# Low parts of the weights by an accumulating DMA instead of a VectorE subtraction

## The chip, the cores and the metric

The kernel runs on one core of one Trainium2 chip. The metric is the device time of one execution in microseconds (us); a verdict compares medians of several runs. The engines are named as the profile names them: PE (TensorE matmul) and PEld (its weight load), DVE (VectorE), ACT (ScalarE), POOL (GpSimd), SP (SyncE, which here issues loads and stores).

## The reference

One inference step of a diffusion backbone with two layers. 128 context tokens and 512 latent tokens go through the same weights. Each layer is a feed-forward sublayer, a token mixer (differential attention in layer 0, a gated linear recurrence called HGRN in layer 1) and a second feed-forward sublayer; each has an RMSNorm before and after it and a modulation (shift, scale, gate) made from `w_mod`. Everything is fp32. What matters here are the products with large weights:

```
D_MODEL = 1024;  FFN_HIDDEN = 2816
def swiglu(h, w_in, w_out):
    a, b = jnp.split(h @ w_in, 2, axis=-1)
    return (jax.nn.silu(a) * b) @ w_out
...
z = h @ w_in                                            # attention 1024 x 3072, HGRN 1024 x 5120
y = o.reshape(B, L, DA_HEADS * DA_DV) @ w_out           # 1024 x 1024, both mixers
```

## The kernel before

The 640 tokens stand as columns, in two groups of NG = 320, and features lie on the 128 partitions. To hold fp32 accuracy with matmuls in the faster fp32r format, each weight w and each activation x is split into a rounded high part and a low part that is the difference. A product is the sum of three: w_hi x_hi and w_hi x_lo (both line 315) and w_lo x_hi (line 320). One matmul covers 128 rows of weight, 128 output columns and 320 tokens.

A `Unit` is a slab of weights with 128 output columns and 1024 rows (896 for most of the FFN's `w_out`), 512 KB (448 KB). A `Job` multiplies a unit with one group or with both: 24 matmuls for each group, in the order 315, 315, 320 for each 128 rows (with both groups each of these twice). Jobs with both groups fill most of the FFNs. Jobs with one group stand where a stage begins or ends: an "FFN head" (`ffn_head`, 16 units, all for group 0 and then for group 1 in reverse), an "FFN tail" (`split`, the last 8 units of `w_out`, group 0 and then group 1), and many of the mixers' products.

A unit passes through three steps. `ensure_dma` (line 231) loads its raw fp32 slab on SP's queue into a ring of RAW_BUFS = 3 tiles `wraw`. `convert` makes the high part by a rounding copy on ACT (line 249) and the low part by a subtraction on DVE (line 250), into a tile `whl` of a ring of HL_BUFS = 3, or into free space of the large tensors H or G ("hosted" units). `prepare` calls `convert` up to AHEAD = 3 jobs before a job needs it, as far as the ring has room. A raw tile is free again when both parts have been made. The loads of `w_mod` for the modulation (line 559) are in the same SP queue.

Between the matmuls stand small steps of the norms: ACT squares (lines 395, 398), DVE adds them up (399), PE sums over partitions (365), DVE takes a reciprocal square root (lines 350 to 360, tiles rs_a and rs_y) and PE spreads it over the partitions (377). ACT and DVE also take the results out of PSUM (748 to 756 in the FFN: silu, product, split of G into its two parts). A scheduler fixes the order of instructions on every engine when the kernel is built; on the chip each engine goes through its own list in order.

Of the kernel before, what the change touches and what calls it, by code (L numbers as in the profile page):

```python
# [9 lines left out]
F32 = mybir.dt.float32  # L10
# [3 lines left out]
AF = mybir.ActivationFunctionType  # L14
ALU = mybir.AluOpType
# [134 lines left out]
class Net:  # L150
# [83 lines left out]
    def convert(self, n):  # L234
        nc = self.nc
        self.ensure_dma(n)
        u = self.units[n]
        if u.host is None:
            t = self.hlp.tile([128, 2, 8, 128], F32R, name="whl", tag="whl")
            u.w = [t[:, r] for r in range(2)]  # L240
        else:
            if u.host[0] == "H":
                self.hosted = [x for x in self.hosted if x.last >= self.cur] + [u]
            t = getattr(self, u.host[0]).rearrange("p r k t -> p r (k t)")
            u.w = [
                t[:, r, u.host[1]:u.host[1] + 1024].rearrange("p (k c) -> p k c", c=128) for r in range(2)
            ]
        nk = u.nk
        nc.scalar.activation(out=u.w[0][:, 0:nk, :], in_=u.raw[:, 0:nk, :], func=AF.Copy)  # L249
        nc.vector.tensor_tensor(  # L250
            out=u.w[1][:, 0:nk, :], in0=u.raw[:, 0:nk, :], in1=u.w[0][:, 0:nk, :].bitcast(F32), op=ALU.subtract
        )
        u.raw = None

# [1167 lines left out]
```

## Time and profile before

| | |
|---|---|
| Runs | 2905.07, 2910.05, 2908.82 us; median 2908.82 us |
| Profiled execution, its own time (span) | 2910.1 us |
| PE busy | 2855.3 us, 98%, 19278 matmuls |
| DVE busy | 1738.7 us, 60% |
| ACT busy | 995.4 us, 34% |
| POOL busy | 0.2 us |
| q1, the queue of the weight loads | 274.89 MB, 31.5% of the 16 DMA engines' time |

The span runs from the first to the last instruction of one profiled execution and is the time that the later sums are made against. "Busy" is the share of it in which an engine executes. A granted clock (PEclk) of 1.00 is TensorE's upper level, 2.4 GHz, and 0.50 the lower, 1.2 GHz.

### The profile page before, as it was taken

The page shows a single profiled execution, that of the slowest core. Times are in us where ns is not written, and L with a number is a line of the kernel's source. Part 1 is how long each engine was busy: PE and PEld are TensorE (multiplying, and loading weights), DVE is VectorE, ACT ScalarE, POOL GpSimd, SP SyncE. Part 2 cuts the span into 40 slices and gives each one's busy share as a digit, 9 for nine tenths or more (in the row PEclk, how much of TensorE's full clock was granted, in tenths as well). Part 3 has the DMA queues.
Part 4 walks back from the last instruction along what each step waited for, and adds up shares of the span by engine and source line. Part 5 has one row for each costly group of instructions (what it writes and reads, how often), then busy time and mean ns, then how long its engine had stood idle before and what let it go on. Part 6 is the DMA issues. An engine that isn't in the chain of part 4 may idle for free.

```text
span 2910.1 us, 46502 instructions
## 1 busy us (share of the span) xinstructions
PE 2855.3 (98%) x19278; PEld 2749.4 (94%) x19278; DVE 1738.7 (60%) x3605; ACT 995.4 (34%) x1949; POOL 0.2 (0%) x4
## 2 busy tenths in 40 slices
PE   7999999999999999999999999999999999999998
PEld 5999999888888999999999999999999999999998
DVE  6755645866677855665773554387677677223334
ACT  4222123455564422212332212243333344222233
POOL 0000000000000000000000000000000000000000
PEclk9999999999999999999999999999999999999999
DMA  8544432211113344454233433321121122222231
GB/s 264 169 152 139 137 106 81 59 34 36 44 50 101 95 139 151 124 159 138 80 115 104 130 104 107 89 60 55 55 59 51 55 61 80 80 80 73 79 87 39
DMA packets 424399, 278.06 MB, mean 96 GB/s; under 512 B 8410, under 2 KB 385788, under 8 KB 424188
## 3 DMA queue, kind: packets, MB, share of 16 engines
q1 hardware_dynamic: 423680, 274.89, 31.5%
q8 instruction: 152, 2.49, 0.3%
q14 instruction: 59, 0.48, 0.1%
q10 hardware_dynamic: 508, 0.20, 0.0%
HBM read 270.34 MB, written 4.72 MB: 95 GB/s over the span
## 4 chain that ended last, share of the span: by engine, by line
PE 91%; DVE 4%; ACT 2%; issue 1%; DMA 1%; ACTq 0%; DVEq 0%; SPq 0%
PE mmps L315 53%; PE mmps L320 26%; PE aux L1258 2%; PE aux L1067 2%; PE aux L1065 1%; PE mmps L1097 1%; PE aux L377 1%; PE aux L626 1%; PE mmps L1086 1%; ACT sq L1329 1%; PE aux L1295 0%; PE aux L365 0%; DVE whl L250 0%; DVE acc L399 0%; DVE rs_a L358 0%
## 5 line engine op out<-in xcount | busy, mean ns | idle before, releaser
L315 PE MATMUL mmps<-H,whl 128*128 128x320 f32 x7232 | 1447.0, 313 | 8.3 <-ACT H L454 6.1
L315 PEld LDWEIGHTS mmps<-H,whl 128*128 128x128 f32 x7232 | 1159.9, 189 | 26.1 <-issue 8.0
L320 PE MATMUL mmps<-H,whl 128*128 128x320 f32 x3616 | 898.0, 312 | 0.3 <-DVE whl L250 0.3
L250 DVE TENSOR_TENSOR whl<-wraw,whl 128x1024 fp32r<-128x1024 f32 (+1 forms) x324 | 387.7, 1197 | 424.0 <-ACT whl L249 422.7
L320 PEld LDWEIGHTS mmps<-H,whl 128*128 128x128 f32 x3616 | 626.3, 189 | 3.0 <-DVE whl L250 0.6
L249 ACT ACTIVATE whl<-wraw 128x1024 fp32r<-128x1024 f32 (+1 forms) x324 | 335.7, 1038 | 594.5 <-issue 369.0
L315 PE MATMUL mmps<-G,whl 128*128 128x320 f32 x2368 | 467.8, 311 | 1.2 <-ACT G L1343 1.2
L315 PEld LDWEIGHTS mmps<-G,whl 128*128 128x128 f32 x2368 | 378.2, 188 | 6.1 <-issue 3.3
L616 DVE SCALAR_TENSOR_TENSOR macc<-wmod,CV,macc 128x512 f32<-128x512 f32 x448 | 307.6, 746 | 0.0
L320 PE MATMUL mmps<-G,whl 128*128 128x320 f32 x1184 | 294.3, 310 | 0.0
L315 PE MATMUL mmps<-G,H 128*128 128x320 f32 x960 | 216.5, 312 | 0.0
L748 ACT ACTIVATE sa<-mmps 128x320 f32<-128x320 f32 x176 | 69.1, 435 | 427.9 <-PE mmps L320 427.8
L753 DVE TENSOR_TENSOR gm<-sa,mmps 128x320 f32<-128x320 f32 x176 | 79.2, 484 | 217.2 <-PE mmps L320 216.5
L320 PEld LDWEIGHTS mmps<-G,whl 128*128 128x128 f32 x1184 | 204.5, 188 | 0.1
L315 PEld LDWEIGHTS mmps<-G,H 128*128 128x128 f32 x960 | 160.7, 188 | 0.5
L320 PE MATMUL mmps<-G,H 128*128 128x320 f32 x480 | 149.7, 312 | 0.0
L837 DVE TENSOR_TENSOR Y<-Y,mmps 128x320 f32<-128x320 f32 x144 | 66.7, 484 | 133.3 <-PE mmps L320 133.3
L315 PE MATMUL mmps<-H,G 128*128 128x320 f32 x448 | 103.4, 312 | 0.0
L835 ACT ACTIVATE Y<-mmps 128x320 f32<-128x320 f32 x96 | 38.5, 435 | 180.3 <-PE mmps L320 180.0
L399 DVE TENSOR_TENSOR acc<-acc,sq 128x320 f32<-128x320 f32 x168 | 80.2, 487 | 20.3 <-ACT sq L398 18.9
L320 PEld LDWEIGHTS mmps<-G,H 128*128 128x128 f32 x480 | 90.3, 188 | 0.4
L997 DVE TENSOR_REDUCE sm<-aux 128x1 f32<-128x640 f32 x64 | 52.7, 824 | 53.9 <-PE aux L1067 53.8
(222 smaller groups left out, 2540.3 us busy)
## 6 DMA issues: line engine op xcount, KB each, us to landing
wraw<-in_ffn_w_in SPq DMA_DIRECT2D x192, 512.0 KB, 3.9
wmod<-in_w_mod SPq DMA_DIRECT2D x66, 1024.0 KB, 5.6
wraw<-in_ffn_w_out SPq DMA_DIRECT2D x64, 448.0 KB, 3.9
wraw<-in_hgrn_w_in SPq DMA_DIRECT2D x40, 512.0 KB, 3.9
wraw<-in_ffn_w_out SPq DMA_DIRECT2D x32, 512.0 KB, 4.1
wraw<-in_attn_w_in SPq DMA_DIRECT2D x24, 512.0 KB, 4.0
wm<-in_w_mod SPq DMA_DIRECT2D x4, 1024.0 KB, 11.5
wraw<-in_attn_w_out SPq DMA_DIRECT2D x8, 512.0 KB, 4.1
```

The costliest lines, as they stand in the source:

```text
L249: nc.scalar.activation(out=u.w[0][:, 0:nk, :], in_=u.raw[:, 0:nk, :], func=AF.Copy)
L250: nc.vector.tensor_tensor(out=u.w[1][:, 0:nk, :], in0=u.raw[:, 0:nk, :], in1=u.w[0][:, 0:nk, :].bitcast(F32), op=ALU.subtract)
L315: nc.tensor.matmul(out=ps[g][:, 0:NG], lhsT=w[0][:, a, :], rhs=rhs[:, r, b, g * NG:(g + 1) * NG], start=(i == 0 and r == 0), stop=False,)
L320: nc.tensor.matmul(out=ps[g][:, 0:NG], lhsT=w[1][:, a, :], rhs=rhs[:, 0, b, g * NG:(g + 1) * NG], start=False, stop=(i == last),)
L399: return lambda: nc.vector.tensor_tensor(out=acc, in0=acc, in1=sq, op=ALU.add)
L616: nc.vector.scalar_tensor_tensor(out=acc[s], in0=w, scalar=cv, in1=acc[s], op0=ALU.mult, op1=ALU.add)
L748: nc.scalar.activation(out=st[g], in_=ps, func=AF.Silu)
L753: nc.vector.tensor_tensor(out=t, in0=st[g], in1=ps, op=ALU.mult)
L837: nc.vector.tensor_tensor(out=y, in0=y, in1=ps, op=ALU.add)
L997: nc.vector.tensor_reduce(out=sm[:, c:c + 1], in_=x, axis=AX.X, op=ALU.max)
L1067: nc.tensor.matmul(out=o, lhsT=QL[r, qc], rhs=KH[r, c, k0:k1], start=False, stop=True)
L1258: nc.tensor.matmul(out=ps[:, c * 128:(c + 1) * 128], lhsT=km[:, c * 128:(c + 1) * 128], rhs=self.view(Q2, c * 128, dims), start=True, stop ...
```

## The change

`convert` makes the low part in two new steps. ACT writes a second copy of the raw slab, rounded in the same way and negated, into the place of the low part. Then POOL issues a DMA from the raw slab into that place, SBUF to SBUF, which adds what it moves to what is there: raw minus high. DVE's subtraction is gone. Each of the 368 conversions gets both steps; lines below move by two (315 becomes 317, 320 becomes 322, 748 becomes 750, and so on).

```
@@ -247,8 +247,10 @@
         nk = u.nk
         nc.scalar.activation(out=u.w[0][:, 0:nk, :], in_=u.raw[:, 0:nk, :], func=AF.Copy)
-        nc.vector.tensor_tensor(
-            out=u.w[1][:, 0:nk, :], in0=u.raw[:, 0:nk, :], in1=u.w[0][:, 0:nk, :].bitcast(F32), op=ALU.subtract
+        nc.scalar.activation(out=u.w[1][:, 0:nk, :], in_=u.raw[:, 0:nk, :], func=AF.Copy, scale=-1.0)
+        nc.gpsimd.dma_start(
+            out=u.w[1][:, 0:nk, :].rearrange("p k c -> p (k c)"),
+            in_=u.raw[:, 0:nk, :].rearrange("p k c -> p (k c)"), accum_op=ALU.add,
         )
         u.raw = None
```

The build order shows where the new steps stand. This is ACT's list at the first FFN tail (layer 0, first FFN) before the change; `whl<-wraw` and `H<-wraw` are the copies of a ring unit and of a hosted unit, `G<-gm` the split of the FFN's product, `sa<-mmps` the silu, `acc` and `sq` squares for the norm.

```order
L748 ACTIVATE sa<-mmps 128x320 x2
L249 ACTIVATE whl<-wraw 128x1024
L249 ACTIVATE H<-wraw 128x1024 x2
L249 ACTIVATE whl<-wraw 128x1024
L755 ACTIVATE G<-gm 128x320 x2
L249 ACTIVATE H<-wraw 128x1024
```

The same place with the change:

```order
L750 ACTIVATE sa<-mmps 128x320 x2
L249 ACTIVATE whl<-wraw 128x1024
L250 ACTIVATE whl<-wraw 128x1024
L249 ACTIVATE H<-wraw 128x1024
L250 ACTIVATE H<-wraw 128x1024
L249 ACTIVATE whl<-wraw 128x1024
L757 ACTIVATE G<-gm 128x320 x2
L250 ACTIVATE whl<-wraw 128x1024
L249 ACTIVATE H<-wraw 128x1024
```

Every copy has a second one behind it, and for the last ring unit of the tail the two G copies stand between its first and its second copy; one hosted unit now stands ahead of it where two stood.

On SP the raw loads of the following units, at the same tail, with the semaphores that each waits for. Before:

```order
L231 DMA wraw<-in_ffn_w_out 128x8x128 [waits DMAHW7_49,DVE_49]
L231 DMA wraw<-in_ffn_w_out 128x8x128 [waits DMAHW0_49,DVE_49]
L231 DMA wraw<-in_ffn_w_out 128x8x128 [waits DMAHW1_49,DVE_49]
L231 DMA wraw<-in_ffn_w_out 128x8x128 [waits DMAHW3_49,DVE_49]
L231 DMA wraw<-in_ffn_w_out 128x8x128 [waits DMAHW6_49,DMAHW4_49,DVE_49]
```

With the change:

```order
L231 DMA wraw<-in_ffn_w_out 128x8x128 [waits DMAHW7_49,DMASW7_49,Activation_49]
L231 DMA wraw<-in_ffn_w_out 128x8x128 [waits DMAHW0_49,DMASW0_49,Activation_49]
L231 DMA wraw<-in_ffn_w_out 128x8x128 [waits DMAHW1_49,DMASW1_49,Activation_49]
L231 DMA wraw<-in_ffn_w_out 128x8x128 [waits DMAHW3_49,DMAHW5_49,DMASW2_49,Activation_49]
L231 DMA wraw<-in_ffn_w_out 128x8x128 [waits DMAHW2_49,DMASW3_49,Activation_49]
```

A raw tile is now given back by ACT and by a DMA of POOL's (DMASW) and no longer by DVE.

On PE a norm's sum over partitions (365, after the change 367) and its spread (377, after 379) stand closer together. Before, there are 27 rows with 40 matmuls between them, of which these are the first and the last:

```order
L365 MATMUL aux<-ones,acc_93 128x1 x3
L315 MATMUL mmps<-G,H 128x320
L320 MATMUL mmps<-G,H 128x320
...
L320 MATMUL mmps<-G,H 128x320
L315 MATMUL mmps<-G,H 128x320 x2
L377 MATMUL aux<-ident,rs_y 128x128 x2
```

With the change there are 15 rows with 22 matmuls at the same norm:

```order
L367 MATMUL aux<-ones,acc_93 128x1 x3
L322 MATMUL mmps<-G,H 128x320
L317 MATMUL mmps<-G,H 128x320 x2
...
L317 MATMUL mmps<-G,H 128x320 x2
L322 MATMUL mmps<-G,H 128x320
L379 MATMUL aux<-ident,rs_y 128x128 x2
```

Less work of PE now stands between a norm's sum and the spread that needs the square root made from it on DVE.

## Rows read from the trace of the kernel before

**Rows 1.** Page, part 1: busy us, share of the span, instructions.
```profile
PE 2855.3 (98%) x19278; PEld 2749.4 (94%) x19278; DVE 1738.7 (60%) x3605; ACT 995.4 (34%) x1949; POOL 0.2 (0%) x4
```
**Rows 2.** Page, part 4: the chain that ended last, by engine.
```profile
PE 91%; DVE 4%; ACT 2%; issue 1%; DMA 1%; ACTq 0%; DVEq 0%; SPq 0%
```
**Rows 3.** Windows: us, busy by engine, PEclk, DMA share, GB/s; sum of four.
```profile
118.00:450.00 332.00, 332.00 (x2296) 325.95 (x2295) 188.36 (x301) 79.09 (x131) 0.00 (x0) 1.00 0.43 132
...
sum 1367.00, PE 1367.00 PEld 1350.07 DVE 641.98 ACT 322.26 POOL 0.00; mean PE 341.75 PEld 337.52 DVE 160.49 ACT 80.57 POOL 0.00
```
**Rows 4.** Page, part 5: busy us, mean ns of one, idle before, releaser.
```profile
L250 DVE TENSOR_TENSOR whl<-wraw,whl 128x1024 fp32r<-128x1024 f32 (+1 forms) x324 | 387.7, 1197 | 424.0 <-ACT whl L249 422.7
```
**Rows 5.** Page, part 6: DMA issues, KB each, us to landing.
```profile
wraw<-in_ffn_w_in SPq DMA_DIRECT2D x192, 512.0 KB, 3.9
wmod<-in_w_mod SPq DMA_DIRECT2D x66, 1024.0 KB, 5.6
...
wm<-in_w_mod SPq DMA_DIRECT2D x4, 1024.0 KB, 11.5
```
**Rows 6.** Waits of SP's queue: us in total, times, longest.
```profile
SPq L231 <- DVE whl L250: 1585.3, 237, 33.5
```
**Rows 7.** Timeline, both-group jobs: copy and first low-part matmul, w_in and w_out.
```profile
234.15 1.06 ACT L249 ACTIVATE whl<-wraw 128x1024 fp32r<-128x1024 f32 x1
...
248.11 0.46 PE L320 MATMUL mmps<-H,whl 128*128 128x320 f32 x2
...
185.10 1.06 ACT L249 ACTIVATE whl<-wraw 128x1024 fp32r<-128x1024 f32 x1
...
197.31 0.46 PE L320 MATMUL mmps<-H,whl 128*128 128x320 f32 x2
```
**Rows 8.** Timeline, first FFN tail, third ring unit.
```profile
465.58 1.04 ACT L249 ACTIVATE whl<-wraw 128x1024 fp32r<-128x1024 f32 x1
466.52 0.81 ACT L755 ACTIVATE G<-gm 128x320 fp32r<-128x320 f32 x2
...
471.77 0.31 PE L320 MATMUL mmps<-G,whl 128*128 128x320 f32 x1
```
**Rows 9.** Timeline, three units of FFN heads: copy and first low-part matmul.
```profile
969.97 1.05 ACT L249 ACTIVATE whl<-wraw 128x1024 fp32r<-128x1024 f32 x1
...
973.92 0.31 PE L320 MATMUL mmps<-H,whl 128*128 128x320 f32 x1
...
1451.59 2.00 ACT L249 ACTIVATE whl<-wraw 128x1024 fp32r<-128x1024 f32 x2
...
1455.90 0.31 PE L320 MATMUL mmps<-H,whl 128*128 128x320 f32 x1
...
92.89 1.05 ACT L249 ACTIVATE whl<-wraw 128x1024 fp32r<-128x1024 f32 x1
...
99.69 0.31 PE L320 MATMUL mmps<-H,whl 128*128 128x320 f32 x1
```
**Rows 10.** Startup: timeline of ACT and PE, one piece of the chain.
```profile
29.71 1.99 ACT L249 ACTIVATE whl<-wraw 128x1024 fp32r<-128x1024 f32 x2
...
36.08 0.47 PE L320 MATMUL mmps<-H,whl 128*128 128x320 f32 x1
...
60.33 0.41 PE L320 MATMUL mmps<-H,whl 128*128 128x320 f32 x1 [0.33 <-DVE whl L250]
...
59.14 1.14 DVE whl L250
```
**Rows 11.** Two stalls of PE in the timeline, and windows behind them.
```profile
549.60 1.22 PE L377 MATMUL aux<-ident,rs_y 128*128 128x128 f32 x4 [2.57 <-DVE rs_y L360]
...
2447.08 0.56 PE L315 MATMUL mmps<-H,whl 128*128 128x320 f32 x2 [1.29 <-ACT H L454]
...
547.40:557.60 10.20, 6.38 (x22) 5.57 (x23) 8.18 (x36) 4.37 (x13) 0.00 (x0) 0.50 0.00 1
...
2448.60:2452.00 3.40, 3.40 (x15) 3.40 (x15) 3.40 (x12) 2.19 (x6) 0.00 (x0) 0.50 0.00 0
```

## The prediction, written before the changed kernel ran

> **What bounds the kernel now.** I read the page's busy times first: PE is busy for 2855.3 of 2910.1 us, so all its idle time is 54.8 us, while DVE stands at 60% and ACT at 34% [rows 1]. The chain that ended last is PE for 91% and DVE for 4% [rows 2]. Then I went by stage. Four windows that hold only both-group jobs add up to 1367.00 us, and PE is busy in 1367.00 of them at a granted clock of 1.00; in the first the DMA engines are busy for 0.43 of the time [rows 3]. In half the span nothing can be gained, and the change matters only if it makes something late. DVE's subtractions cost 387.7 us in the largest group alone [rows 4], but nearly all of that lies beside PE.
>
> So the question is how long before PE needs a low part the high part's copy ends. I call this the lead: from the end of line 249's copy to the first matmul of line 320 with that unit. I read it unit by unit in the timeline.
>
> - Both-group jobs: a `w_in` unit is copied from 234.15 to 235.21 and its low part is needed at 248.11, a lead of 12.9; for a `w_out` unit it is 197.31 - 186.16 = 11.1 [rows 7]. I counted 144 and 64 such units.
> - FFN tails, third ring unit, the same in all four: 471.77 - 466.62 = 5.15 [rows 8].
> - FFN heads: 973.92 - 971.02 = 2.90; the first of two copies ends near 1452.6, so 1455.90 - 1452.6 = 3.3; and 99.69 - 93.94 = 5.75, which stands for five units of 5.5 to 5.8 [rows 9].
> - Startup: the first of two copies ends near 30.7 and PE needs its low part at 36.08. At 60.33 PE already waits 0.33 us for a subtraction; that unit's copy ends at 55.6 [rows 10].
>
> All other units have leads of 7.7 and more.
>
> **The cost of the new low part.** Before, a low part costs 1.2 us of DVE plus DVE's queue. After, it costs a second copy on ACT, as long as the first, 1.06 us [rows 7], and then the DMA: its issue on POOL, the transfer, and the semaphore. I call the time from the end of the second copy to the landing x; a unit is in time if 1.06 + x is at most its lead. No row shows x, since POOL issues no DMA before. Bounds: the DMA reads a 512 KB operand from SBUF and has to read the 512 KB that it adds to, so not less than a 512 KB load, 3.9; by bytes read, like a 1,024 KB load, 5.6; and when many transfers stand in line, like a 1,024 KB load at startup, 11.5 [rows 5]. I take **x = 7**: 5.6, and a quarter of the way to 11.5, because it shares the engines with the loads. How tight that is: at 132 GB/s the engines are busy for 0.43, so in a 7.05 us job (48 matmuls at 0.147) they move 0.93 MB in 3.0 us, and 512 KB costs 1.7 us of all 16; twice that for an accumulating DMA brings them to 6.4 of 7.05 us [rows 3].
>
> The Trainium skill, "DMA: Bandwidth & Descriptors", section "Anatomy of one DMA — SWDGE (gpsimd) path", fits such a DMA with 2.0 us plus its bytes at 436 GB/s. No run before shows it; an estimate from that page for 1 MB is 4.4 us, and the sum by it would be about +6 instead of what follows. That is the first rival.
>
> **The sum at x = 7, need 8.06.**
> - Tails: 4 x (8.06 - 5.15) = 11.6. In the new order the two G copies (0.73 us from start to start of the next) come between the copies of this unit, but one hosted unit's copy (0.97) that stood ahead of it is gone; I let these cancel. PE's order there is unchanged, so nothing can pass a late low part.
> - Heads: 5.16 + 4.8 + 5 x 2.3 = 21.5.
> - Startup: the first low part lands at 30.7 + 1.06 + 11.5 = 43.3 (loads fill the queues there, so the upper bound) where 36.08 was wanted, 7.2; the one at 60.33 lands at 55.6 + 8.06 = 63.7, 3.3. Three subtractions of 1.13 or 1.14 that are on the chain there, one of which is shown [rows 10], go: -3.4. Together 7.1.
> - Both-group jobs: 8.06 against 11.1 and 12.9, so nothing. This cover is gone from x = 10.
> - ACT: 368 x 1.05 = 386 us more, from 34% to 47%. Where an eviction queues behind a second copy it is 1.06 us late; nothing, because a PSUM bank is wanted again over 2 us after most evictions. If that cover were missing in a fifth of 368 units it would cost up to 70, which I put in the range only.
> - SP: raw loads now wait for the DMA instead of DVE, about 6 us later, and the `w_mod` loads are queued behind them. Loads are issued up to 33.5 us ahead of the subtraction that frees them [rows 6], so this is hidden in the stages; nothing to about x = 9.
> - Norms: between sum and spread there are 22 matmuls, 3.2 us, where 40 stood, 5.9. With nothing between them the square root took 2.57 us of PE's wait [rows 11]. It fits on a DVE that has lost the subtractions: nothing, with 0 to 2 us in each of 24 places as bounds.
> - DVE's relief elsewhere: PE's idle 54.8 us bounds it [rows 1]; taken as nothing beyond the 3.4.
>
> That is 11.6 + 21.5 + 7.1 = 40. To it comes the clock. After a wait of 2.57 us the trace shows 10.2 us at 0.50, after 1.29 us 3.4 us at 0.50 [rows 11]: half of such a stretch, 5.1 and 1.7, is lost again. Nine new stalls of 2.3 to 2.9 at 1.7 and three of 3 to 5 at 3.4, between the two, are 15.3 + 10.2 = 25.5. The profiled execution would take 2910.1 + 40 + 25.5 = 2976; it lies 1.3 above the median, so I predict **2975 us**. From x = 5.6 (40 becomes 22, the clock 10) to x = 9 (85, the clock 35) the likeliest case's own range is 2940 to 3030.
>
> **Rivals.** About 0.2% (6 us) is what can be told from no change.
>
> 1. *Hidden, not slower.* The add is free and the pieces of 4 KB a row move quicker than a load's: x is 4.4 or less. Then tails cost 4 x 0.3 = 1.2, heads 2.6 + 2.2, startup nothing after the relief: 2910 to 2916. For it: 0.57 of the DMA engines' time is free in the stages [rows 3]. Against it: two 512 KB operands and an issuer never seen here. It decides at x = 4.4. A variant, faster: the freed DVE shortens norms and startup, 2895 to 2903. Against: DVE is 4% of the chain [rows 2], and the tight heads lose more.
> 2. *The steady stages break.* x is 11 or more, alone or because the engines are full (6.4 of 7.05 us is close). Each conversion starts when a job ends and serves the job after next, so a job grows by half of what is late: at x = 12, 144 x 0.08 + 64 x 0.98 = 74, tails 31.6, heads 56, startup 13, clock 40: about 3125. At x = 14, 155 + 127 + 40 + 71 + 17 and clock 45: about 3360.
> 3. *The queue on ACT and the new order.* x is small but second copies delay evictions and the square root comes late: up to 24 x 2 = 48 and the 70 above, about 2940 to 3000. Against it: the slack of over 2 us.
>
> The Trainium skill, "Collectives: The Full Stack", section "The bandwidth ceiling: the fold count and why AG ≠ RS ≠ AR", says that the add itself costs no cycles but that its second source read halves the rate. No run before shows it; it is what the first rival would have in its favour and the doubled bytes in mine.
>
> **How the numbers follow.** Forecast 0.52, rival 1 0.16 (0.12 same, 0.04 faster), rival 2 0.22, rival 3 0.10. Both others above it and the forecast are slower: faster 0.04, same 0.12, slower 0.84. The range leaves out the faster variant and part of "same" below, and the upper half of rival 2 above: 2914 to 3240.
>
> **What would show it.** PE waits at line 322 for whl by a DMA, about 12 times, 2 to 5 us each, at tails and heads, with half-speed stretches behind; both-group windows stay at PE busy throughout; accumulating DMAs land about 7 us after issue; ACT near 47%, DVE near 45%; DMA share in the stages towards 0.9. The prediction is wrong if waits at 322 stand in the both-group windows (rival 2), if none stands at the heads (rival 1), or if PE's new waits name ACT's evictions or rs_y (rival 3).

## The result and the profile after

The changed kernel takes 2981.56 us (median of 4 runs, 2974.3 to 2988.91), the kernel before 2909.44 (median of 4). The ratio is 1.0244, with a 95% interval of 1.0223 to 1.0265: slower by 2.4%. The prediction was 2975. The profiled execution spans 2977.1 us, 67.0 more than before.

The page of the changed kernel: busy times, the DMA queue that POOL's accumulating DMAs use (packets, MB, share of 16 engines), the chain, the group of low-part matmuls, and the DMA issues (KB, us to landing).

```profile
PE 2880.3 (97%) x19278; PEld 2764.8 (93%) x19278; DVE 1327.9 (45%) x3237; ACT 1328.2 (45%) x2317; POOL 317.5 (11%) x372
...
q0 software_dynamic: 52992, 188.77, 34.4%
...
PE 79%; DMA 8%; ACT 4%; issue 4%; DVE 4%; SPq 0%; POOL 0%; ACTq 0%; DVEq 0%; POOLq 0%
...
L322 PE MATMUL mmps<-H,whl 128*128 128x320 f32 x3616 | 898.2, 312 | 15.5 <-DMA whl<-wraw 13.3
...
whl<-wraw POOLq DMA_DIRECT2D x260, 512.0 KB, 5.3
...
wmod<-in_w_mod SPq DMA_DIRECT2D x66, 1024.0 KB, 8.0
```

Read beside [rows 1, 2, 5]: DVE lost 411 us and ACT gained 333, which moves nothing by itself, since neither is the bound. PE's idle time grew from 54.8 to 2977.1 - 2880.3 = 96.8 us (+42.0), and its busy time by 25.0 for the same 19278 matmuls. The two make the 67.0. The `w_mod` loads take 8.0 us instead of 5.6: the new DMAs share the engines with them.

Who PE waits for (us in total, times, longest):

```profile
PE mmps L322 <- DMA whl<-wraw: 23.5, 13, 3.7
PE aux L367 <- DVE acc L401: 9.4, 5, 2.7
...
PE mmps L322 <- ACT sq L400: 5.3, 2, 3.3
...
PE aux L379 <- DVE rs_y L362: 3.4, 3, 1.6
PE mmps L322 <- DMA H<-wraw: 3.4, 4, 1.9
...
PE mmps L322 <- DMA G<-wraw: 2.4, 1, 2.4
PE mmps L322 <- ACT acc L397: 2.2, 1, 2.2
...
PE mmps L322 <- ACT whl L250: 1.1, 1, 1.1
...
PE mmps L322 <- ACT whl L249: 1.0, 1, 1.0
```

The same view of the kernel before has these two lines for its line 320:

```profile
PE mmps L320 <- DVE whl L250: 0.3, 1, 0.3
...
PE mmps L320 <- DVE G L250: 0.2, 1, 0.2
```

DMAs of low parts are named 18 times, with 29.3 us. At the five waits of line 322 put down to ACT, too, the unit's DMA landed within 0.2 us before the matmul, so these are waits for a low part as well. Every unit's DMA matched to the matmul that waits for it gives 23 waits at the 368 units, 39.0 us in all, where 0.5 stood before. That is nearly the whole of the 42.0 us that PE's idle time grew.

One of them is the tail of [rows 8], the third ring unit, in the timelines of ACT, POOL and PE:

```profile
481.16 1.06 ACT L249 ACTIVATE whl<-wraw 128x1024 fp32r<-128x1024 f32 x1
482.12 0.82 ACT L757 ACTIVATE G<-gm 128x320 fp32r<-128x320 f32 x2
482.84 1.04 ACT L250 ACTIVATE whl<-wraw 128x1024 fp32r<-128x1024 f32 x1
...
484.18 0.86 POOL L251 DMA_DIRECT2D whl<-wraw  x1 [1.96 <-ACT whl L250]
...
491.34 0.38 PE L322 MATMUL mmps<-G,whl 128*128 128x320 f32 x1 [2.94 <-DMA whl<-wraw]
```

The second copy ends at 483.88, POOL issues at 484.18, the data is there at 491.2 (x = 7.3), and PE, which would have been ready at 488.4, starts at 491.34.

### The profile page after: what moved, and what is told of

Its sections match the earlier page's. It is cut to its first block, busy times and chain, and to the rows that moved or that the text cites. A ratio compares the mean times of both kernels' runs of the same rounds, so it can differ in the third digit from the quotient of the medians.

```text
span 2977.1 us, 47828 instructions
## 1 busy us (share of the span) xinstructions
PE 2880.3 (97%) x19278; PEld 2764.8 (93%) x19278; DVE 1327.9 (45%) x3237; ACT 1328.2 (45%) x2317; POOL 317.5 (11%) x372
## 4 chain that ended last, share of the span: by engine, by line
PE 79%; DMA 8%; ACT 4%; issue 4%; DVE 4%; SPq 0%; POOL 0%; ACTq 0%; DVEq 0%; POOLq 0%
PE mmps L317 45%; PE mmps L322 23%; DMA whl<-wraw 3%; PE aux L1260 2%; DMA wraw<-in_ffn_w_in 2%; DMA wraw<-in_ffn_w_out 2%; PE aux L1069 2%; PE aux L1067 1%; DMA H<-wraw 1%; PE mmps L1099 1%; PE aux L628 1%; DMA G<-wraw 1%; PE aux L379 1%; ACT sq L1331 1%; PE aux L1297 0%
## 5 line engine op out<-in xcount | busy, mean ns | idle before, releaser
L249 ACT ACTIVATE whl<-wraw 128x1024 fp32r<-128x1024 f32 (+1 forms) x324 | 336.4, 1038 | 523.5 <-issue 331.1
L251 POOL DMA_DIRECT2D whl<-wraw x324 | 279.5, 863 | 2342.3 <-ACT whl L250 1990.2
L250 ACT ACTIVATE whl<-wraw 128x1024 fp32r<-128x1024 f32 (+1 forms) x324 | 333.9, 1030 | 0.0
L322 PE MATMUL mmps<-G,whl 128*128 128x320 f32 x1184 | 296.5, 312 | 12.5 <-DMA whl<-wraw 10.3
L317 PEld LDWEIGHTS mmps<-G,H 128*128 128x128 f32 x960 | 162.7, 190 | 0.6
L616 DVE TENSOR_SCALAR macc<-wmod,CV 128x512 f32<-128x512 f32 x64 | 30.4, 483 | 226.7 <-PE aux L628 226.6
L758 DVE TENSOR_TENSOR G<-gm,G 128x320 fp32r<-128x320 f32 x176 | 80.1, 488 | 75.0 <-ACT G L757 74.4
```

The source lines that it names most:

```text
L250: nc.scalar.activation(out=u.w[1][:, 0:nk, :], in_=u.raw[:, 0:nk, :], func=AF.Copy, scale=-1.0)
L251: nc.gpsimd.dma_start(out=u.w[1][:, 0:nk, :].rearrange("p k c -> p (k c)"), in_=u.raw[:, 0:nk, :].rearrange("p k c -> p (k c)"), accum_op= ...
L317: nc.tensor.matmul(out=ps[g][:, 0:NG], lhsT=w[0][:, a, :], rhs=rhs[:, r, b, g * NG:(g + 1) * NG], start=(i == 0 and r == 0), stop=False,)
L322: nc.tensor.matmul(out=ps[g][:, 0:NG], lhsT=w[1][:, a, :], rhs=rhs[:, 0, b, g * NG:(g + 1) * NG], start=False, stop=(i == last),)
L758: nc.vector.tensor_tensor(out=self.tv(self.G[:, 1, jj, :], g), in0=t, in1=hi.bitcast(F32), op=ALU.subtract)
```

## The experiments

My theory after the result: the loss is the time from the high part's copy to the landing of the DMA, at the units with a short lead, with a lower clock behind some of the waits. The rivals: the load on the 16 DMA engines in the long stages, and ACT's second copies with the order they force.

**The DMA replaced by an addition on DVE.**

```
-        nc.gpsimd.dma_start(out=low, in_=raw, accum_op=ALU.add)
+        nc.vector.tensor_tensor(out=low, in0=raw, in1=low, op=ALU.add)
```

> One half of the change alone: ACT's negated second copy stays, but DVE adds the raw slab to it instead of the DMA (no accumulating DMA is left). If the loss comes from the latency of the DMA at units with a short lead (my theory), this is near the kernel before: 2908 to 2922 us, with waits for whl of about 1 us at a few places where DVE was just in time, at startup above all. If ACT's 386 us of second copies and the new order of its list are what costs (rival), it stays above 2945 us.

Measured: 2932.48 us, ratio to before 1.0069 (1.0053 to 1.0086). Neither range held. A second copy that DVE must wait for costs about 20 us, somewhat over half of what I gave the rival as its least, but not nothing. The largest single piece is at startup, in the timelines of ACT, DVE and PE:

```profile
59.02 1.05 ACT L250 ACTIVATE whl<-wraw 128x1024 fp32r<-128x1024 f32 x1
...
61.63 1.22 DVE L251 TENSOR_TENSOR whl<-wraw,whl 128x1024 fp32r<-128x1024 f32 x1
...
62.90 0.63 PE L321 MATMUL mmps<-H,whl 128*128 128x320 f32 x1 [3.80 <-DVE whl L251]
```

The negated copy ends at 60.07, and DVE, in its own order, gets to the addition at 61.63. In [rows 10] PE waited 0.33 us at this place.

**A DMA that copies and does not add.**

```
-            in_=raw, accum_op=ALU.add,
+            in_=raw,
```

> The changed kernel, but the DMA copies and does not add: the low part is then the raw slab itself, so the values differ and only the time counts. If the add costs the engines a second read (my term for x), the DMA's landing falls from 5.3 us to about 4 and its queue's share of the 16 engines from 34% to about 20%; with x some 1.5 us shorter at about 25 places the time falls to 2940 to 2960 us. If the latency is fixed cost of issue and completion and the add is free (rival), landing stays at 5 and more and the time at 2975 to 2985 us.

Measured: 2922.18 us, ratio 1.0037 (1.0024 to 1.005). The DMA landed in 3.0 us where 5.3 stood (the page's median for ring units), and its queue fell to this share:

```profile
q0 software_dynamic: 52992, 188.77, 18.8%
...
whl<-wraw POOLq DMA_DIRECT2D x260, 512.0 KB, 3.0
```

The same packets and bytes cost 0.188 x 2921.8 / 368 = 1.49 us of all 16 engines for each DMA, and 0.344 x 2977.1 / 368 = 2.78 us with the add: 1.9 times. The rival of a free add falls. My own range was missed as well, on the other side: I took 1.5 us off x at each wait, but x fell by 2.0 (its median over all units from 5.67 to 3.64), and a wait vanishes altogether once its lead is long enough; 11 waits for a low part were left, with 14.4 us, of the 23 with 39.0. This run isolates the add: PE, ACT, DVE and POOL have the same instructions in the same order as in the changed kernel. The add alone is thus 2981.56 - 2922.18 = 59 us of the loss, and the second copies, the new order and a plain DMA together cost 9.9 us net.

**New low parts only far from single-group jobs, and only near them.**

```
+        single = {pos[id(j.unit)] for j in self.jobs if len(j.groups) == 1}
+            u.near = any(i - d in single for d in range(4))      # for the i-th unit
...
+        if u.near:            # the second kernel: if not u.near
+            (subtraction on DVE as before)
+        else:
             (negated copy and accumulating DMA)
```

> The new low parts only for 226 units far from single-group jobs (leads of 11 and more); the 142 units of single-group jobs and the three after each such unit keep DVE's subtraction. My theory: all of the 226 are hidden, 2903 to 2916 us, no wait of PE for whl by a DMA above 1 us. Rival (the DMA engines are shared by loads and adds, so that loads are late everywhere): 2930 us or more.

> The opposite: the new low parts only for the 142 units near single-group jobs. My theory: nearly the whole loss is there, 2955 to 2985 us, with 18 or more waits of PE for a DMA into whl, H or G. Rival (load on the DMA engines in the long stages): 2920 to 2940 us.

Measured: 2912.74 us for the 226 far units (ratio 1.0004, 0.9995 to 1.0014), and 2980.27 us for the 142 near ones (1.0237, 1.0211 to 1.0263). In the near-only kernel 16 waits of PE name a DMA of a low part and four more at the same line an instruction of ACT; I had expected 18 or more. The whole loss lies with the near units; the far ones cost nothing, although the DMA engines are busy for 0.83 of a long stage. A window of both-group jobs in the far-only kernel, to be read beside [rows 3]:

```profile
118.00:450.00 332.00, 332.00 (x2295) 325.95 (x2295) 134.75 (x254) 123.05 (x179) 41.49 (x48) 1.00 0.83 205
```

PE is busy throughout at 1.00, with DVE down from 188 to 135 us. That this relief gains nothing follows as well: the far-only kernel is not faster than before.

**The add issued twice for the far units.**

```
             nc.gpsimd.dma_start(out=low, in_=raw, accum_op=ALU.add)
+            nc.gpsimd.dma_start(out=low, in_=raw, accum_op=ALU.add)
```

> The kernel that uses the new low parts only for the 226 units far from single-group jobs, but with the accumulating DMA issued twice, the second waiting for the first (the low part then holds the raw slab once too often; only the time counts). It asks from where the cover of the long stages is gone. By latency, x is about 12.5: (13.6 - 12.9) / 2 x 144 + (13.6 - 11.1) / 2 x 64 = 130, so 3010 to 3090 us. By the time of the 16 engines (rival), 3.0 us of loads and 2 x 2.8 of adds in a job of 7.05 us: 208 x 1.5 = 320, above 3150 us. If the cover is larger than I read, below 2930 us.

Measured: 3242.7 us, ratio 1.1141 (1.1124 to 1.1158): 330 more than the kernel with one add, where the count by engine time gave 320 and the one by latency 130. Two windows of the first FFN, and the matmuls of the last window of [rows 3] with the new kernel's times:

```profile
160.00:220.00 60.00, 48.77 (x308) 46.59 (x307) 10.49 (x17) 17.53 (x28) 12.26 (x14) 0.94 0.98 222
280.00:340.00 60.00, 46.73 (x291) 45.13 (x290) 15.79 (x29) 15.93 (x24) 10.53 (x13) 0.93 0.96 229
...
2751.36:3155.96 404.60, 364.68 (x2402) 353.55 (x2401) 42.59 (x91) 128.66 (x189) 85.72 (x98) 1.00 0.92 189
```

In the first FFN the DMA engines are busy for 0.96 and more, and PE for 0.8. The matmuls of the four windows of [rows 3] take 92, 100, 75 and 53 us longer than in the far-only kernel, nearly the whole loss, at a DMA share of 0.92 to 0.95. That the engines are close to full is shown; that their time alone sets the loss is not, and the 320 is partly luck. It took the loads of the first window for all four. The last one has fewer loads:

```profile
2478.00:2830.00 352.00, 352.00 (x2402) 352.00 (x2402) 99.67 (x141) 83.95 (x141) 0.00 (x0) 1.00 0.27 78
...
2478.00:2830.00 352.00, 352.00 (x2402) 352.00 (x2401) 43.43 (x91) 128.89 (x189) 42.17 (x49) 1.00 0.63 147
```

The first line is the kernel before, the second the far-only kernel: one add took 0.36 of the engines, and a second would bring them to 0.99, so no growth by engine time, where 53 us were measured. Counted like this the four windows would grow by about 190. And x, to the landing of the second DMA, was 14.6 to 17.9 us (medians by window) where I had taken 12.5, so it had passed the leads of 11.1 and 12.9 as well. The run does not separate the two limits. The changed kernel, at 0.85 and 0.86 in its first two windows, is not far from full.

**The low part first.**

```
-        nc.scalar.activation(out=high, in_=raw, func=AF.Copy)
         nc.scalar.activation(out=low, in_=raw, func=AF.Copy, scale=-1.0)
         nc.gpsimd.dma_start(out=low, in_=raw, accum_op=ALU.add)
+        nc.scalar.activation(out=high, in_=raw, func=AF.Copy)
```

> The changed kernel with the two copies of ACT exchanged: the negated copy and the DMA first, the high part's copy behind them. x (6.75 us in the middle at the 30 units where PE waits) stays, the low part is ready about 1.05 us sooner, the high part later by as much. My theory: some 25 waits lose about 1 us each and the clock behind them half as much, 2940 to 2962 us. Rival: the high part becomes what PE waits for at line 317, 2970 to 2990 us.

Measured: 2951.24 us, ratio 1.0143 (1.0127 to 1.016), 30 less than the changed kernel, as my theory had it, and PE does not wait for a high part at 317. The waits for `whl` at 322 went from 23.5 to this:

```profile
PE mmps L322 <- DMA whl<-wraw: 16.0, 14, 3.7
```

**The DMA in two halves.**

```
-        nc.gpsimd.dma_start(out=low, in_=raw, accum_op=ALU.add)
+        for k0, k1 in ((0, nk // 2), (nk // 2, nk)):
+            nc.gpsimd.dma_start(out=low[:, k0:k1], in_=raw[:, k0:k1], accum_op=ALU.add)
```

> The changed kernel with the accumulating DMA in two halves of 256 KB, the half that PE uses first in front. If most of the landing time of 5.3 us grows with the bytes, the first half lands 1 to 2 us sooner and the time falls to 2945 to 2968 us. If it is fixed per DMA (rival), or if POOL's issue of 0.86 us for each counts, 2978 to 3010 us.

Measured: 2972.25 us, ratio 1.0214 (1.0194 to 1.0233). It lies between the two ranges: some 9 us better than the changed kernel, with runs that overlap (2970.08 to 2976.03 against 2974.3 to 2988.91). The page's median landing of a half, 5.0 us, mixes the two: the first half lands 4.3 us after its issue, 1.1 sooner than the whole, the second 6.1 us after the issue of the first, 0.8 later than the whole. POOL's busy time doubles to 645.7 us.

**A spare copy on ACT in the kernel before**, which nothing reads: made from the raw slab, and in a second kernel from the high part.

```
         nc.scalar.activation(out=u.w[0], in_=u.raw, func=AF.Copy)
+        nc.scalar.activation(out=spare, in_=u.raw[:, 0:6], func=AF.Copy, scale=-1.0)     # the second: in_=u.w[0][:, 0:6]
```

> The kernel before with one more copy on ACT in each conversion (768 of the 1024 columns, negated, into a spare tile that nothing reads), behind the high part's copy; DVE still subtracts. It asks what ACT's occupation costs by itself, apart from the low part that waits for it. My theory: hidden, 2908 to 2918 us. Rival (late evictions and a new order): 2925 us and more, as in the kernel with ACT's copy and DVE's addition, which took 20 us more than before.

> The kernel before with one more copy on ACT in each conversion, as in the run with a spare copy, but made from the high part that was just copied instead of the raw slab (768 columns, 0.84 us, into a tile that nothing reads), so that it cannot be moved ahead of the high part's copy and wait there for a load. My theory: ACT's occupation alone is hidden, 2908 to 2918 us, with no wait of PE for ACT's G above 2 us. Rival (late evictions and the changed order cost by themselves): 2925 to 2950 us, as the two runs with a second copy showed.

Measured: 2947.0 us (ratio 1.0132, 1.0093 to 1.0172) from the raw slab, and 2917.31 us (1.003, 1.002 to 1.0041) from the high part. The first does not answer its question. Its copies had been placed ahead of the high part's copy, which needs room in the ring, and stood there until the raw slab landed; for the spare copy's line, the idle time of ACT ahead of it and what ended it (us, times):

```profile
  DMA wraw<-in_ffn_w_in: 534.5, 155
  DMA wraw<-in_ffn_w_out: 340.3, 78
```

What stood behind them on ACT was late: PE waited 10.5 us for three splits of G (L757). The second kernel cannot do this, and shows the price of occupying ACT alone, with copies of three quarters of the length: about 9 us, close to the upper end of what I gave it.

**Hosted units by DVE**, all others as in the changed kernel.

```
+        if u.host is not None:
+            (subtraction on DVE as before)
+        else:
             (negated copy and accumulating DMA)
```

> The changed kernel, but the 44 units hosted in H and G keep DVE's subtraction. In the changed kernel PE waited 8.7 us for hosted units of the FFN tails and 2.4 us for one in G at startup, which my sum did not have. If their own DMAs and the raw tiles these hold are the cause, these waits go, with half as much of clock behind them: 2960 to 2970 us. If the tail is late as a whole (rival), other units take the waits over: 2974 to 2985 us.

Measured: 2951.47 us, ratio 1.0149 (1.0132 to 1.0166): 30 less, more than I expected. No wait for a hosted unit is left, and the page has these busy times:

```profile
PE 2865.3 (97%) x19278; PEld 2752.1 (93%) x19278; DVE 1375.9 (47%) x3281; ACT 1290.2 (44%) x2273; POOL 280.1 (10%) x328
```

PE's idle time fell by 15.6 to 81.2 and its busy time by 15.0. The third ring units of the tails still wait, but for 1.15, 2.30, 3.42 and 1.56, 8.4 us in all where it was 11.5. That fits fewer DMAs on the engines in the tails, but one of the four grew, and I did not test it apart.

**Both remedies.**

```
+        if u.host is not None:
+            (high part's copy, subtraction on DVE as before)
+        else:
             (negated copy, accumulating DMA, then the high part's copy)
```

> Both remedies in one kernel: the 44 hosted units keep DVE's subtraction, the other 324 have the negated copy and the accumulating DMA ahead of the high part's copy. Each alone took 30 us off the changed kernel (to 2951). If the loss is a sum of separate late low parts, the 14 waits for a DMA that were left (25.8 us) shrink by about 1 us each and the clock with them: 2925 to 2938 us. If both remedies relieve the same waits (rival), 2945 to 2955 us. It is not expected to beat the kernel before.

Measured: 2939.6 us, ratio 1.0085 (1.0065 to 1.0105). Just above my range: two gains of 30 us together make 42, so part of them is the same waits. No version here beats the kernel before.

## Why the prediction was right, step by step

The time was 67.0 us over the profiled execution of before where the sum had 40 + 25.5 = 65.5. The total is closer than its parts, and part of that is luck. The stated range, 2914 to 3240, would have held almost any slower kernel; what bears the mechanism out is where PE waits. I expected about 12 waits of 2 to 5 us at tails and heads: there were 23, nine of them of 2 us and more, all but one at the tails, the heads and startup.

- **x.** Taken as 7. Over all units its median is 5.7, close to the 5.6 of the 1,024 KB row; at the 23 units where PE waits it is 6.8. It runs from 4.5 to 11.9, so all but one unit lie within the bounds of 3.9 and 11.5. The reason given for the surcharge, shared engines, fits this spread but was not tested by itself. From the issue on POOL to the landing it is 5.3 and not the 7 that I named as a sign.
- **Tails.** 11.6 predicted for the third ring unit, 2.94 + 3.68 + 2.20 + 2.67 = 11.5 measured. Here too parts cancel, as I had let them: in the new order the leads are 6.2, 5.3, 6.2 and 6.2 instead of 5.15, but with the two G copies in between the second copy ends 1.67 us after the first and not 1.06. Missing in the sum were the hosted units behind it: 8.7 us in three of the four tails. I had put a late raw slab off to x = 9. A raw slab for a hosted unit waits for a raw tile, and that is now held until the DMA has landed; in the third tail ACT waits 9.41 us for one and PE then 3.31:

```profile
1931.13 1.06 ACT L249 ACTIVATE H<-wraw 128x1024 fp32r<-128x1024 f32 x1 [9.41 <-DMA wraw<-in_ffn_w_out]
...
1933.43 0.86 POOL L251 DMA_DIRECT2D H<-wraw  x1 [10.92 <-ACT H L250]
...
1938.10 0.61 PE L322 MATMUL mmps<-G,H 128*128 128x320 f32 x1 [3.31 <-ACT sq L400]
```

  The waits of SP's queue (us, times, longest) name these DMAs among those that hold raw loads back:

```profile
SPq L231 <- DMA H<-wraw: 136.7, 27, 8.4
```

- **Heads.** 21.5 predicted, 10.4 measured in eight waits of 0.61 to 2.48. I read the leads from the trace of before, but the build order of the changed kernel is another one and gives these units more. The counterpart of the 2.90 in [rows 9] shows it, in the timelines of ACT and PE:

```profile
989.45 1.05 ACT L249 ACTIVATE whl<-wraw 128x1024 fp32r<-128x1024 f32 x1
...
992.14 1.04 ACT L250 ACTIVATE whl<-wraw 128x1024 fp32r<-128x1024 f32 x1
...
998.82 0.41 PE L322 MATMUL mmps<-H,whl 128*128 128x320 f32 x1 [1.45 <-DMA whl<-wraw]
```

From the copy's end at 990.50 to the matmul without its wait, at 997.37, are 6.9 us, although the second copy starts only 1.6 us after the first has ended. This term and the hosted units' are errors of 11 and 9 us that cancel.
- **Startup.** 7.1 predicted; the waits at 322 there are 3.12, 0.38, 2.44 and 1.52, together 7.5, where 0.33 stood.
- **Both-group jobs.** Nothing predicted, and the far-only kernel confirms it. In the changed kernel one wait stands there, at the unit with the longest x, 11.9:

```profile
1758.80 0.53 PE L322 MATMUL mmps<-G,whl 128*128 128x320 f32 x2 [1.00 <-DMA whl<-wraw]
```

  Taken by its letter, my sign for the second rival (a wait at 322 in the both-group windows) appeared, once and for 1.00 us. At this unit x had passed the bound "x = 10"; its median over all units, 5.7, stayed far below. The count of 6.4 of 7.05 us is near the share of 0.85 in the changed kernel (6.0).
- **ACT.** Nothing predicted; occupying ACT alone costs about 9 us. A second copy with DVE's wait for it costs 20, but that wait is not in the changed kernel. Its own order with a plain DMA costs 9.9 us net, and in that waits for the DMA are still included. ACT's busy time rose by 333 us, not 386: copies that follow each other overlap in the profile (two take 2.00 in [rows 9]).
- **Norms.** Nothing predicted. The waits of the sum and the spread add up to 9.4 + 3.4 = 12.8 where 4.6 + 3.4 + 2.7 = 10.7 stood before, +2.
- **The clock.** 25.5 predicted, and PE's busy time grew by 25.0, but not as I had it, with a slow stretch behind every wait. Behind the wait of 2.94 us the clock stayed at 1.00; behind one of 3.68 it was low for a while:

```profile
491.40:498.00 6.60, 6.60 (x45) 6.60 (x46) 0.00 (x0) 0.83 (x1) 0.00 (x0) 1.00 1.08 247
...
1422.90:1433.00 10.10, 10.10 (x51) 10.10 (x52) 1.50 (x4) 5.26 (x7) 1.57 (x2) 0.71 0.93 225
```

Over the whole span, time times the part of the clock that was missing is 33.7 us before and 52.7 after: 19 of the 25. About 5 of the other 6 lie in how busy time is counted: in a row of matmuls the next one starts 0.15 us later, but the last before a wait counts with its whole 0.31, and PE's row breaks for more than 0.1 us 84 times where it was 54. So the 25.5 came out by luck. Its price was also read too high: the 10.2 us in [rows 11] begin during the wait itself, and PE is busy for only 6.38 of them.
- **The range.** The 85 at x = 9 is more than the leads listed give: tails 19.6, heads 35.5 and startup 9.1 make 64.

Of the rivals, the hidden one fails by the add: with a plain copy it would have been nearly right. The breaking stages did not come, and are one more add away. ACT's queue and the new order come, net of DVE's relief, to at most about 10 us of the 72 between the medians, by the kernel with the plain DMA; the 59 us of the add are nearly all of the rest.

The Trainium skill, "Collectives: The Full Stack", section "The bandwidth ceiling: the fold count and why AG ≠ RS ≠ AR", has the add of a ReduceScatter as a second source read that halves the rate, and not as cycles. Here it took 1.9 times the engine time and 2.0 us more to land (medians over all units), which agrees. "DMA: Bandwidth & Descriptors", section "Anatomy of one DMA — SWDGE (gpsimd) path", gives by its fit an estimate of 3.2 us for 512 KB and of 4.4 for 1 MB; measured were 3.3 without and 5.3 with the add as medians over all units, and 4.5 as the shortest of 512 KB with it. So the estimate for the plain DMA agrees, and the one for doubled bytes is near the shortest and 0.9 us under the median; how much of that comes from the loads beside it, no run here separates.

## What to carry to other kernels

Work that moves off a half-idle engine gains nothing where another engine is the bound; what counts is how long before its use the result is there. So list, unit by unit, the time from what it is made of to its first use, and compare the new latency, its longest cases too, with the shortest of these, not with the average. Read the leads from the new build order where a scheduler makes it, and count for DMAs both their latency at short leads and their engine time in the long stages.

## What the runs showed that I had not expected

An accumulating DMA also costs more to issue: 0.86 us on POOL for each, 0.53 for the same DMA without the add. The issuing line's row in the changed kernel (ns from shortest over median to longest, first and last start):

```profile
L251 POOL DMA_DIRECT2D whl<-wraw x324: 859/859/1113, 32.2 to 2894.8; - x162
```

The same row of the kernel whose DMA does not add:

```profile
L251 POOL DMA_DIRECT2D whl<-wraw x324: 527/528/662, 30.5 to 2843.6; - x162
```

Two adds in a row turned a hidden cost into 330 us: the first FFN, which showed no wait at a DMA share of 0.83, lost a fifth of PE's time at 0.96.
